# One room for the value products, halves added on load, inverse sums by VectorE: a change to a one-layer hybrid encoder step on Trainium2

## The chip, the cores and the metric

The kernel runs on one core of a Trainium2 chip. A core has TensorE (PE, with its weight loads shown apart as PEld), VectorE (DVE), ScalarE (ACT), GpSimd (POOL) and SyncE (SP, which here only issues transfers), an on-chip memory of 128 partitions (SBUF), the matmul accumulators (PSUM, eight banks), and 16 DMA engines to and from DRAM. The metric is the time of one execution in microseconds (us) on the device; lower is better. Time before: 1430.43 us, median of three runs (1429.32 to 1431.48).

## The reference

One inference step of one layer, for a prompt of 1024 rows and a sample of 64 rows, width 1024, all in fp32:

```
xn = rms_norm(x, g_pre);  z = xn @ w_in          # xa, ga, q, k, v, gb, fl, ma, mb
ya = rg_lru(causal_conv(xa)) * silu(ga)                        # branch A
logf = log_sigmoid(fl + b_f);  cum = cumsum(logf)
s  = q @ k.T * HEAD_DIM**-0.5 + cum[q] - cum[k], masked        # branch B, 16 heads of 64
yb = (softmax(s) @ v) * silu(gb)
u  = [ya, yb] @ w_branch;  mix = sum(sigmoid([ma, mb]) * u) @ w_o
h  = x + rms_norm(mix, g_post)
y  = h + rms_norm(sigmoid(h @ w_ple_gate) * (pe @ w_ple_proj), g_ple)
```

The sample attends to 128 cached rows and itself. Besides y, the step returns k, v, logf and the end states of branch A.

## The kernel before

**Precision.** A matmul operand is split into a high part, rounded to the fast matmul format, and a low part, the remainder. A product takes three passes (high x high, high x low, low x high; lines 179 to 181). ScalarE makes the high part (`copy_act`, line 90), VectorE the low part (`sub`, line 93), so nearly every operand passes both engines, in that order. In the value products of attention, a weight tile holds a value block's high columns (64) beside its low columns (64), so that one pass of 128 output partitions gives "high values" in the lower 64 and "low values" in the upper 64; the two halves have to be added afterwards.

**Stages.** (1) norm, value columns, (2) keys, queries and some other panels by a seven-product scheme (`quad`), (3) attention, mixed with panel products as filler, (4) branch A (convolution, gates, scan), (5) output product of branch A, while branch B's rows come back from DRAM, (6) output product of branch B, (7) w_o, again by seven products, and the last norm and gate.

**Attention.** There are 64 units, each a head and 256 queries (two blocks of 128, called `par` 0 and 1). For a unit:
- `scores` (two matmuls per piece) and `lowest`: VectorE adds the mask and takes the negated maximum,
- `softmax`: ScalarE's exponential with its row sums `sm` (line 1191), GpSimd's power -1 of the sums (line 1193), GpSimd's scaling of the row (line 1194),
- `turn`: four transposes on PE, then ScalarE's high part `th` and VectorE's low part `tl`,
- `values`: matmuls into one half `pv` of a PSUM bank. `pv_half` hands out the two halves of that one bank in turn. After a unit's last value product ScalarE copies the upper 64 partitions to `lo`, VectorE adds the lower 64 from PSUM to it (`y`, line 1293), and GpSimd's queue stores y to DRAM `d_y` (line 1297).

For each of 8 head pairs the sample goes the same way (`sample_scores`, `sample_turn`, `sample_values`): two small copies and two adds out of `pv`, store by SP.

**The order** in attention is worked out while the program is built. PE's instructions are issued in program order, and within attention so are those of ScalarE, VectorE and GpSimd. A planner keeps a clock `now` for PE and, per engine, a list of booked work with estimated costs (the constants `D_MAX`, `A_LO`, `D_Y`, `G_INV`, ...). Of the next score, transpose and value step it takes the first whose due time plus a margin has come (`ready`, `MARGIN`); if there is none it issues one step of a filler panel. The due time of a unit's first value product is also that of a free half: `v_free`, with two entries, one per half. In all other stages PE keeps program order and the other engines' order is worked out by a scheduler when the program is built.

**Branch B's rows.** After attention, `branch_in` (line 1818) loads for each of 8 row blocks k the 128 x 1088 rows `t` of d_y and the rows `z` of d_gb, by SP. `branch_b` gates them: ScalarE's sigmoid of z, VectorE's t * z and t * sigmoid, ScalarE's high part `ybh`, VectorE's low part `ybl`. Rows 0 and 1 are loaded early, before branch A's last scan; rows 2 to 7 share two buffers, so row k + 2 is loaded when row k's low part is done. In the same stage `evac_a` multiplies branch A's products by a gate and stores them to `d_mix` on GpSimd's queue (line 1865, four buffers), and weight panels are loaded by SP and split. Branch B's first panel needs all eight rows within its first 24 matmuls.

Of the kernel before, what the change touches and what calls it, by code (L numbers as in the profile page):

```python
# [8 lines left out]
F32 = mybir.dt.float32  # L9
# [29 lines left out]
GC = 364  # L39

HOP_PE, HOP = 250.0, 90.0
D_MAX, D_LO, D_Y, D_YS = (240.0, 1.035), (130.0, 1.1), 420.0, 230.0
A_EXP, A_HI, A_LO, A_ST, A_W = (450.0, 0.85), (150.0, 0.88), 380.0, 470.0, 1060.0
G_NORM, G_INV = (260.0, 0.84), 220.0
G_DMA = 860.0
D_W = 1240.0

# [26 lines left out]
def hybrid_step(tc, a, o):  # L74
# [958 lines left out]
    def spent(ns):  # L1033
        now[0] += ns
# [21 lines left out]
    def per(cost, n):  # L1056
        return cost[0] + cost[1] * n
# [120 lines left out]
    def tiny2(name):  # L1178
        return p2.tile([P, 1], F32, name=name, tag=name, bufs=12 if name == "nm" else 8)[:, :]

    def lowest(s, w, out, m, least=-NEG):

# [1 line left out]
        return nm, book("D", now[0] + HOP_PE, per(D_MAX, w), lambda: dve.tensor_tensor_reduce(  # L1184
            out=out, in0=s[:, :w], in1=m, scale=-1.0, scalar=least, op0=ALU.add, op1=ALU.min, accum_out=nm))

    def softmax(at, nm, n, pr):


        sm = tiny2("sm")  # L1190
        at = book("A", at, per(A_EXP, n), lambda: act.activation(  # L1191
            out=pr[:, :n], in_=pr[:, :n], func=AF.Exp, scale=-1.0, bias=nm, accum_out=sm))
        at = book("G", at, G_INV, lambda: pool.tensor_tensor(out=sm, in0=sm, in1=warm[:, :], op=ALU.pow))  # L1193
        return book("G", at, per(G_NORM, n), lambda: pool.tensor_scalar(  # L1194
            out=pr[:, :n], in0=pr[:, :n], scalar1=sm, scalar2=1.0, op0=ALU.mult, op1=ALU.mult))

    def width(q2, par):
        n = 256 * q2 + (par + 1) * P
# [4 lines left out]
    def scores(x, i, pr):  # L1203

        h, q2 = units[x]
        t = heads[h]
        half, par = divmod(i, 2)
        n, w = width(q2, par)
        q0 = (2 * q2 + par) * P
        c = slice(half * w, (half + 1) * w)  # L1210
        s = p2s.tile([P, 512], F32, name="s", tag="s")
        pe.matmul(s[:, :w], t["q1"][:, q0:q0 + P], t["k1"][:, c], start=True, stop=False)  # L1212
        pe.matmul(s[:, :w], t["q2"][:HD + 4, q0:q0 + P], t["k2"][:HD + 4, c], start=False, stop=True)  # L1213
        spent(logits_ns(w))
# [39 lines left out]
    lo_free = [0.0]  # L1254
    def values(u, g, h, q2):
        vv = heads_v[h]
        if g == 0:
            pvs[u] = pv_half()
        pv = pvs[u]
        th, tl = turned.pop((u, g))  # L1260
        high = turned_by.pop((u, g))
        def part(j, x, **kw):
            v = vv[:, 2 * g + j, :, :].rearrange("p s d -> p (s d)")
            if g < q2:
                return pe.matmul(pv[:, :256], v, x[:, j * 256:(j + 1) * 256], **kw)  # L1265
            c0 = P if j else 0
            return pe.matmul(pv[:, c0:256], v, x[:, :P] if j else x[:, P:3 * P], **kw)  # L1267

        def high_part(j, stop=False):
            tc.declare_no_dep(part(j, th, start=False, stop=stop).ins, high.ins, reason="ordered through the low part")  # L1270

        if g < q2:
            for j in range(2):
                part(j, tl, start=(g == 0 and j == 0), stop=False)
                high_part(j)
            spent(480.0)
            return
        if q2 == 0:
            part(0, tl, start=True, stop=False)
# [12 lines left out]
        at = book("A", max(now[0] + HOP_PE, lo_free[0]), A_LO, lambda: copy_act(lo[:, :], pv[HD:, :256]))  # L1292
        at = book("D", at, D_Y, lambda: dve.tensor_tensor(out=y[:, :], in0=pv[:HD, :256], in1=lo[:, :], op=ALU.add))
        v_free.popleft()
        v_free.append(at)
        lo_free[0] = at
        book("G", at, G_DMA, lambda: pool.dma_start(dst, y[:, :]))


# [10 lines left out]
    def sample_scores(p):  # L1310
        t = smp[p]
        s = p2s.tile([P, 512], F32, name="s", tag="s")
        three(s[:, :LS], *(x[:, :] for x in qs + t["ks"]), True, False)
        pe.matmul(s[:, :LS], cs_q[:, :], cs_k[:, :], start=False, stop=True)
        spent(440.0)
        nm, at = lowest(s, LS, prs_s[:, :LS], mask_s[:, :])
        return at, softmax(at, nm, LS, prs_s)

    def sample_turn(p):
        t = smp[p]  # L1320
# [9 lines left out]
    def sample_values(p):  # L1330
        t = smp.pop(p)
        pv = pv_half()
        for i in range(2):
            pe.matmul(pv[:, :], t["vs"][:, i, 0, :], t["pt"][:, i, :, :].rearrange("p s n -> p (s n)"),
                      start=(i == 0), stop=False)
            pe.matmul(pv[:, :P], t["vs"][:, i, 1, :], t["pt"][:, i, 0, :], start=False, stop=(i == 1))
        spent(458.0)
        ys = p2.tile([P, DEC], F32, name="ys", tag="ys", bufs=1)
        ats = []
        for j in range(2):  # L1340
            js, ks = slice(j * HD, (j + 1) * HD), slice(P + j * HD, P + (j + 1) * HD)
            ats.append(book("A", now[0] + HOP_PE, per(A_HI, HD), lambda js=js, ks=ks: copy_act(ys[js, :], pv[js, ks])))
        for j, at in enumerate(ats):
            js = slice(j * HD, (j + 1) * HD)
            at = book("D", at, D_YS, lambda js=js: dve.tensor_tensor(out=ys[js, :], in0=pv[js, js], in1=ys[js, :],
                                                                     op=ALU.add))
# [25 lines left out]
    due = {}  # L1372
    s_free = deque([0.0, 0.0, 0.0])
    t_free = deque([0.0, 0.0])
    v_free = deque([0.0, 0.0])
    prs = {}
    seen = {"t": 0, "v": 0}
    last_t = {u: ("t", u, q2) for u, (h, q2) in enumerate(units)}
# [62 lines left out]
            t_free.append(due[step])  # L1441
        done.add(step)

    pool.memset(warm[:, :], -1.0)
    booking = tc.manual_schedule(engines={act.engine, dve.engine, pool.engine})
    booking.__enter__()
    load_head(0)
# [369 lines left out]
        return ybpool.tile([P, T], dt, name=name, tag=f"yb{i}{k}")  # L1817

    def branch_in(k, t, z):
        sp.dma_start(t[:, :], d_y[k])  # L1820
        sp.dma_start(z[:, :], d_gb[k])
        return t, z

# [574 lines left out]
```

## Time and profile before

| | us |
|---|---|
| median of three runs | 1430.43 (1429.32 to 1431.48) |
| the profiled execution | 1429.49 |
| its span, first to last instruction | 1427.5 |
| PE busy | 1410.8 |
| PEld busy | 1358.0 |
| VectorE busy | 899.4 |
| ScalarE busy | 720.5 |
| GpSimd busy | 436.5 |
| granted TensorE clock | 0.998 |

Attention runs from about 453 to 849 us of the span, branch A until about 1046, the output product of branch A with the loading of branch B's rows until about 1111. Busy times of one engine are unions, so a busy PE is one with work in its pipeline. In a row of waits, the instruction named first waited, and the one behind the arrow ended the wait. In a row of time order, the bracket tells how long the engine had been idle before it and what ended that.

### The profile page before, as it was taken

To read this page: it belongs to the slowest core of one execution; us is meant where nothing else is said; L and a number is where in the kernel's file an instruction comes from. 1 tells how busy PE (TensorE), PEld (TensorE's weight loads), DVE (VectorE), ACT (ScalarE), POOL (GpSimd) and SP (SyncE) were. 2 spreads that over 40 slices of the span, in tenths; PEclk is the share of its full clock that TensorE was granted. 3 is DMA by queue.
4 is the path that set the end of the run, shared out by engine and by line. 5 is a ranking of instruction groups with operands and counts; after the bars stand their busy time and mean duration, and the time that the engine had idled before them with its cause. 6 is when DMAs were issued, how large, how long until landed. Compare 5 with 4: busy or idle time off the path is not lost.

```text
span 1427.5 us, 25022 instructions
## 1 busy us (share of the span) xinstructions
PE 1410.8 (99%) x9217; PEld 1358.0 (95%) x9217; DVE 899.4 (63%) x1638; ACT 720.5 (50%) x1339; POOL 436.5 (31%) x652
## 2 busy tenths in 40 slices
PE   9999999999999999999999999999999999999997
PEld 8999999999999999999999999999999999888887
DVE  5564766564432666666666656898767474777654
ACT  5423544442222666666666657777544232565443
POOL 0012322233204777768776841221011000000001
PEclk9999999999999999999999999999999999999999
DMA  6667556765247764556566545564467774224211
GB/s 225 214 133 107 150 155 193 162 180 141 85 122 194 182 130 131 137 110 151 123 150 131 84 101 106 83 101 84 165 211 264 252 237 136 113 74 150 78 48 45
DMA packets 138919, 201.20 MB, mean 141 GB/s; under 512 B 24372, under 2 KB 98844, under 8 KB 137772
## 3 DMA queue, kind: packets, MB, share of 16 engines
q1 hardware_dynamic: 119436, 158.96, 44.2%
q0 software_dynamic: 8160, 23.25, 5.9%
q10 hardware_dynamic: 11200, 17.38, 3.4%
q8 instruction: 73, 1.20, 0.3%
q14 instruction: 50, 0.41, 0.1%
HBM read 131.60 MB, written 66.36 MB: 139 GB/s over the span
## 4 chain that ended last, share of the span: by engine, by line
PE 82%; DVE 6%; DMA 5%; ACT 3%; issue 3%; POOL 1%; SPq 0%; DVEq 0%; ACTq 0%; POOLq 0%
PE quad L844 17%; PE acc L179 11%; PE acc L181 11%; PE acc L180 11%; PE q L2042 5%; PE tp L1244 4%; PE pv L1265 3%; PE s L1213 2%; PE s L1212 2%; PE pv L1267 2%; PE vacc L179 1%; PE vacc L180 1%; PE vacc L181 1%; DMA w_raw<-in_w_in 1%; PE vacc L500 1%
## 5 line engine op out<-in xcount | busy, mean ns | idle before, releaser
L179 PE MATMUL acc<-xh,wh 128*128 128x364 f32 x720 | 237.6, 330 | 0.2 <-ACT st L90 0.2
L181 PE MATMUL acc<-xh,wl 128*128 128x364 f32 x720 | 235.8, 328 | 0.0
L180 PE MATMUL acc<-xl,wh 128*128 128x364 f32 x720 | 235.8, 327 | 0.0
L179 PEld LDWEIGHTS acc<-xh,wh 128*128 128x128 f32 x720 | 135.4, 188 | 1.2 <-ACT st L90 0.5
L180 PEld LDWEIGHTS acc<-xl,wh 128*128 128x128 f32 x720 | 135.3, 188 | 0.8
L181 PEld LDWEIGHTS acc<-xh,wl 128*128 128x128 f32 x720 | 135.1, 188 | 0.0
L90 ACT ACTIVATE wh<-w_raw 128x1024 fp32r<-128x1024 f32 (+1 forms) x66 | 63.4, 962 | 86.4 <-PE quad L844 34.4
L93 DVE TENSOR_TENSOR wl<-w_raw,wh 128x1024 fp32r<-128x1024 f32 (+1 forms) x55 | 62.5, 1138 | 67.6 <-ACT wh L90 47.0
L1193 POOL TENSOR_TENSOR sm<-sm,warm 128x1 f32<-128x1 f32 x136 | 79.2, 582 | 57.0 <-ACT pb L1191 21.8
L93 DVE TENSOR_TENSOR tl<-tp,th 128x512 fp32r<-128x512 f32 x96 | 65.6, 687 | 38.7 <-ACT th L90 37.9
L844 PE MATMUL quad<-xh,wh 128*128 128x272 f32 x416 | 87.4, 291 | 1.8 <-ACT p__3330 L90 1.8
L844 PE MATMUL quad<-xl,wh 128*128 128x272 f32 x416 | 86.1, 288 | 0.0
L844 PE MATMUL quad<-xh,wl 128*128 128x272 f32 x416 | 86.0, 288 | 0.0
L1191 ACT ACTIVATE pb<-pb,nm 128x896 f32<-128x896 f32 (+1 forms) x64 | 63.3, 989 | 24.0 <-DVE nm L1184 21.3
L90 ACT ACTIVATE th<-tp 128x512 fp32r<-128x512 f32 x96 | 56.4, 592 | 31.0 <-PE tp L1244 30.3
L2338 POOL TENSOR_TENSOR junk<-ple,g_ple 128x256 f32<-128x256 f32 x4 | 3.8, 956 | 213.2 <-DVE ple L2295 213.2
L1212 PE MATMUL s<-k,q 128*128 128x128 f32 (+2 forms) x192 | 67.5, 353 | 0.0
L844 PEld LDWEIGHTS quad<-xh,wh 128*128 128x128 f32 x416 | 65.3, 188 | 2.3 <-ACT p__3330 L90 2.0
L1213 PE MATMUL s<-k,q 68*128 68x128 f32 (+2 forms) x192 | 65.3, 344 | 0.5 <-issue 0.5
L844 PEld LDWEIGHTS quad<-xh,wl 128*128 128x128 f32 x416 | 65.5, 188 | 0.0
L844 PEld LDWEIGHTS quad<-xl,wh 128*128 128x128 f32 x416 | 65.4, 188 | 0.0
L1194 POOL TENSOR_SCALAR pb<-pb,sm 128x896 f32<-128x896 f32 (+1 forms) x64 | 61.5, 962 | 6.2
(744 smaller groups left out, 4230.4 us busy)
## 6 DMA issues: line engine op xcount, KB each, us to landing
w_raw<-in_w_in SPq DMA_DIRECT2D x56, 256.0 KB
q<-d_q SPq DMA_DIRECT2D x48, 256.0 KB
k<-d_k SPq DMA_DIRECT2D x48, 256.0 KB
w_raw<-in_w_in SPq DMA_DIRECT2D x64, 128.0 KB
w_raw<-in_w_branch SPq DMA_DIRECT2D x32, 256.0 KB
wl<-w_raw POOLq DMA_DIRECT2D x11, 512.0 KB, 4.5
wraw<-in_w_in SPq DMA_DIRECT2D x20, 256.0 KB
d_k<-oh ACTq DMA_DIRECT2D x16, 272.0 KB
```

The source lines that it names most:

```text
L90: return act.activation(out=out, in_=in_, func=AF.Copy, scale=scale)
L93: return eng.tensor_tensor(out=out, in0=in0, in1=in1, op=ALU.subtract)
L179: pe.matmul(out, ah, bh, start=start, stop=False)
L180: pe.matmul(out, ah, bl, start=False, stop=False)
L181: pe.matmul(out, al, bh, start=False, stop=stop)
L844: pe.matmul(acc[:, c, :CW], l[:, k, :], r[:, k, c * CW:(c + 1) * CW], start=(first and k == 0 and p == 0), stop=(k == 3 and p == 2), skip_ ...
L1191: at = book("A", at, per(A_EXP, n), lambda: act.activation(out=pr[:, :n], in_=pr[:, :n], func=AF.Exp, scale=-1.0, bias=nm, accum_out=sm))
L1193: at = book("G", at, G_INV, lambda: pool.tensor_tensor(out=sm, in0=sm, in1=warm[:, :], op=ALU.pow))
L1194: return book("G", at, per(G_NORM, n), lambda: pool.tensor_scalar(out=pr[:, :n], in0=pr[:, :n], scalar1=sm, scalar2=1.0, op0=ALU.mult, op1 ...
L1212: pe.matmul(s[:, :w], t["q1"][:, q0:q0 + P], t["k1"][:, c], start=True, stop=False)
L1213: pe.matmul(s[:, :w], t["q2"][:HD + 4, q0:q0 + P], t["k2"][:HD + 4, c], start=False, stop=True)
L2042: pe.matmul(acc, l[:, k, :], r[:, k, :], start=(first and k == 0 and i == 0), stop=(k == 3 and i == 2), skip_group_check=not first)
```

## The change

- The planner has one entry for the values' bank (`v_free` with one element). After a unit's last value product one ScalarE copy of 128 x 256 empties it into `y`, and the add on VectorE is gone. GpSimd's queue stores both halves, 128 x 256, to `d_y`, which now has a plane of 128 x 1024 per head.
- In `branch_in` two loads on SP bring the lower halves of the two heads, one brings the sample's rows from `d_ys`, and then two transfers from GpSimd's queue add the upper halves onto the lower ones in SBUF as they land.
- The sample's values are emptied by the same copy, and its two adds read SBUF.
- The sums of a unit's two rows stand side by side in one tile of two columns. After the second exponential one VectorE reciprocal inverts both, and GpSimd then scales the first row and the second. For the sample it inverts one column.
- The planner's costs follow (`INV` 165, `A_Y` 380; `D_Y`, `A_LO`, `G_INV` go).

```
-    d_y = dram.tile([NP, P, T], F32, name="d_y")
+    d_y = dram.tile([NP, 2, P, SEQ], F32, name="d_y")
+    d_ys = dram.tile([NP, P, DEC], F32, name="d_ys")
...
-    def softmax(at, nm, n, pr):
-        sm = tiny2("sm")
-        at = book("A", at, per(A_EXP, n), lambda: act.activation(
+    def powers(at, nm, n, pr, sm):
+        return book("A", at, per(A_EXP, n), lambda: act.activation(
             out=pr[:, :n], in_=pr[:, :n], func=AF.Exp, scale=-1.0, bias=nm, accum_out=sm))
-        at = book("G", at, G_INV, lambda: pool.tensor_tensor(out=sm, in0=sm, in1=warm[:, :], op=ALU.pow))
+    def inverse(at, sm, k):
+        return book("D", at, INV, lambda: dve.reciprocal(out=sm[:, :k], in_=sm[:, :k]))
+    def normal(at, n, pr, sm):
         return book("G", at, per(G_NORM, n), lambda: pool.tensor_scalar(
             out=pr[:, :n], in0=pr[:, :n], scalar1=sm, scalar2=1.0, op0=ALU.mult, op1=ALU.mult))
...
-        return at, softmax(at, nm, n, pr)
+        if par == 0:
+            sm = tiny2("sm", 2)
+            sums[x] = sm, powers(at, nm, n, pr, sm[:, :1]), pr, n
+            return at, at
+        sm, first, pr0, n0 = sums.pop(x)
+        done_ = inverse(max(first, powers(at, nm, n, pr, sm[:, 1:])), sm, 2)
+        return at, normal(normal(done_, n0, pr0, sm[:, :1]), n, pr, sm[:, 1:])
...
-        lo = p2.tile([HD, 256], F32, name="lo", tag="lo", bufs=1)
-        y = p2.tile([HD, 256], F32, name="y", tag="y", bufs=3)
-        dst = d_y[h // 2][(h % 2) * HD:(h % 2 + 1) * HD, q2 * 256:(q2 + 1) * 256]
-        at = book("A", max(now[0] + HOP_PE, lo_free[0]), A_LO, lambda: copy_act(lo[:, :], pv[HD:, :256]))
-        at = book("D", at, D_Y, lambda: dve.tensor_tensor(out=y[:, :], in0=pv[:HD, :256], in1=lo[:, :], op=ALU.add))
+        y = p2.tile([P, 256], F32, name="y", tag="y", bufs=3)
+        dst = d_y[h // 2, h % 2][:, q2 * 256:(q2 + 1) * 256]
+        at = book("A", now[0] + HOP_PE, A_Y, lambda: copy_act(y[:, :], pv[:, :256]))
         v_free.popleft()
         v_free.append(at)
-        lo_free[0] = at
         book("G", at, G_DMA, lambda: pool.dma_start(dst, y[:, :]))
...
-            ats.append(book("A", now[0] + HOP_PE, per(A_HI, HD), lambda js=js, ks=ks: copy_act(ys[js, :], pv[js, ks])))
-        for j, at in enumerate(ats):
-            js = slice(j * HD, (j + 1) * HD)
-            at = book("D", at, D_YS, lambda js=js: dve.tensor_tensor(out=ys[js, :], in0=pv[js, js], in1=ys[js, :],
-                                                                     op=ALU.add))
-        book("D", at, 0.0, lambda: sp.dma_start(d_y[p][:, SEQ:], ys[:, :]))
+            at = book("D", at, D_YS, lambda js=js, ks=ks: dve.tensor_tensor(
+                out=ys[js, :], in0=yv[js, js], in1=yv[js, ks], op=ALU.add))
+        book("D", at, 0.0, lambda: sp.dma_start(d_ys[p], ys[:, :]))
...
-    v_free = deque([0.0, 0.0])
+    v_free = deque([0.0])
...
     def branch_in(k, t, z):
-        sp.dma_start(t[:, :], d_y[k])
+        for j in range(2):
+            sp.dma_start(t[j * HD:(j + 1) * HD, :SEQ], d_y[k, j][:HD, :])
+        sp.dma_start(t[:, SEQ:], d_ys[k])
+        for j in range(2):
+            pool.dma_start(t[j * HD:(j + 1) * HD, :SEQ], d_y[k, j][HD:, :], accum_op=ALU.add)
         sp.dma_start(z[:, :], d_gb[k])
         return t, z
```

More of the change, by code (lines that the diff above doesn't have):

```diff
@@ L41 @@
 HOP_PE, HOP = 250.0, 90.0
-D_MAX, D_LO, D_Y, D_YS = (240.0, 1.035), (130.0, 1.1), 420.0, 230.0
-A_EXP, A_HI, A_LO, A_ST, A_W = (450.0, 0.85), (150.0, 0.88), 380.0, 470.0, 1060.0
-G_NORM, G_INV = (260.0, 0.84), 220.0
+D_MAX, INV, D_LO, D_YS = (240.0, 1.035), 165.0, (130.0, 1.1), 230.0
+A_EXP, A_HI, A_Y, A_ST, A_W = (450.0, 0.85), (150.0, 0.88), 380.0, 470.0, 1060.0
+G_NORM = (260.0, 0.84)
 G_DMA = 860.0
@@ L1176, in load_sample, with tiny2 @@
         t["vs_at"] = book("G", at, 740.0, lambda: sub(pool, vs[:, :, 1, :], v_smp[:, :, :], f(vs[:, :, 0, :])))
-    def tiny2(name):
-        return p2.tile([P, 1], F32, name=name, tag=name, bufs=12 if name == "nm" else 8)[:, :]
+    def tiny2(name, n=1):
+        return p2.tile([P, n], F32, name=name, tag=name, bufs=12 if name == "nm" else 8)[:, :]
     def lowest(s, w, out, m, least=-NEG):
@@ L1185, in lowest @@
             out=out, in0=s[:, :w], in1=m, scale=-1.0, scalar=least, op0=ALU.add, op1=ALU.min, accum_out=nm))
-    def softmax(at, nm, n, pr):
-        sm = tiny2("sm")
-        at = book("A", at, per(A_EXP, n), lambda: act.activation(
+    def powers(at, nm, n, pr, sm):
+        return book("A", at, per(A_EXP, n), lambda: act.activation(
             out=pr[:, :n], in_=pr[:, :n], func=AF.Exp, scale=-1.0, bias=nm, accum_out=sm))
-        at = book("G", at, G_INV, lambda: pool.tensor_tensor(out=sm, in0=sm, in1=warm[:, :], op=ALU.pow))
+    def inverse(at, sm, k):
+        return book("D", at, INV, lambda: dve.reciprocal(out=sm[:, :k], in_=sm[:, :k]))
+    def normal(at, n, pr, sm):
         return book("G", at, per(G_NORM, n), lambda: pool.tensor_scalar(
             out=pr[:, :n], in0=pr[:, :n], scalar1=sm, scalar2=1.0, op0=ALU.mult, op1=ALU.mult))
+    sums = {}
     def width(q2, par):
@@ L1253, in hybrid_step @@
     pvs = {}
-    lo_free = [0.0]
     def values(u, g, h, q2):
@@ L1316, in sample_scores @@
         nm, at = lowest(s, LS, prs_s[:, :LS], mask_s[:, :])
-        return at, softmax(at, nm, LS, prs_s)
+        sm = tiny2("sm", 2)[:, :1]
+        return at, normal(inverse(powers(at, nm, LS, prs_s, sm), sm, 1), LS, prs_s, sm)
     def sample_turn(p):
@@ L1337, in sample_values @@
         spent(458.0)
+        yv = p2.tile([P, 256], F32, name="y", tag="y", bufs=3)
         ys = p2.tile([P, DEC], F32, name="ys", tag="ys", bufs=1)
-        ats = []
+        at = book("A", now[0] + HOP_PE, A_Y, lambda: copy_act(yv[:, :], pv[:, :256]))
+        v_free.popleft()
+        v_free.append(at)
         for j in range(2):
             js, ks = slice(j * HD, (j + 1) * HD), slice(P + j * HD, P + (j + 1) * HD)
-            ats.append(book("A", now[0] + HOP_PE, per(A_HI, HD), lambda js=js, ks=ks: copy_act(ys[js, :], pv[js, ks])))
-        for j, at in enumerate(ats):
-            js = slice(j * HD, (j + 1) * HD)
-            at = book("D", at, D_YS, lambda js=js: dve.tensor_tensor(out=ys[js, :], in0=pv[js, js], in1=ys[js, :],
-                                                                     op=ALU.add))
-        book("D", at, 0.0, lambda: sp.dma_start(d_y[p][:, SEQ:], ys[:, :]))
-        v_free.popleft()
-        v_free.append(at)
+            at = book("D", at, D_YS, lambda js=js, ks=ks: dve.tensor_tensor(
+                out=ys[js, :], in0=yv[js, js], in1=yv[js, ks], op=ALU.add))
+        book("D", at, 0.0, lambda: sp.dma_start(d_ys[p], ys[:, :]))
     units = [(h, q2) for h in range(NH) for q2 in (0, 3, 1, 2)]
@@ L1442, in go @@
         done.add(step)
-    pool.memset(warm[:, :], -1.0)
     booking = tc.manual_schedule(engines={act.engine, dve.engine, pool.engine})
```

## The prediction

> **What bounds the kernel now.** I read the page first, then the busy times by stage, then who waits for whom inside the two stages that the change touches.
>
> ```profile
> PE 1410.8 (99%) x9217; PEld 1358.0 (95%) x9217; DVE 899.4 (63%) x1638; ACT 720.5 (50%) x1339; POOL 436.5 (31%) x652
> ```
>
> ```profile
> 453.00:849.00 396.00, 394.38 (x2739) 383.66 (x2740) 251.19 (x671) 256.14 (x588) 282.18 (x460) 1.00 0.58 131
> 849.00:1046.00 197.00, 196.83 (x1187) 196.53 (x1186) 162.06 (x164) 136.70 (x190) 35.04 (x75) 1.00 0.50 102
> 1046.00:1118.00 72.00, 71.78 (x432) 71.44 (x431) 42.44 (x53) 25.32 (x25) 13.03 (x24) 1.00 0.78 261
> ```
>
> The columns of the second view are the stretch, its length, then busy time (and instructions) of PE, PEld, DVE, ACT and POOL, the granted clock, the DMA share and GB/s. The first row is attention, where score, transpose and value products run with panel products as filler between them. The third is where the output products of branch A run while branch B's rows come back from DRAM and are gated. PE idles 1.62 us in the first and 0.22 us in the third, at full clock. No matmul is added or removed, so the change can win only what PE waits for, and lose by making PE wait. What DVE, POOL and ACT save is worth nothing by itself: none is over 72% busy in attention, and PE's waits there have these names.
>
> ```profile
> PEld pv L1265 <- DVE y L1293: 2.1, 4, 0.7
> PEld pv L1267 <- DVE y L1293: 1.4, 4, 0.4
> PEld pv L1267 <- ACT lo L90: 0.2, 1, 0.2
> PEld pv L1265 <- DVE ys L1345: 0.2, 1, 0.2
> ```
>
> Weight loads run ahead of matmuls, so the wait shows at PEld more fully than at PE (us in total, times, longest). All ten stand at a value product that waits until the values' bank has been emptied: 3.5 us for y, 3.9 us in all. One of them in order of time:
>
> ```profile
> 504.63 0.38 ACT L90 ACTIVATE lo<-pv 64x256 f32<-64x256 f32 x1
> 505.91 0.28 PE L1265 MATMUL pv<-th,vv 128*128 128x256 f32 x1
> 506.29 0.42 DVE L1293 TENSOR_TENSOR y<-pv,lo 64x256 f32<-64x256 f32 x1 [1.95 <-ACT st L90]
> 506.75 0.19 PEld L1267 LDWEIGHTS pv<-diag0l,vv 128*128 128x128 f32 x1 [0.36 <-DVE y L1293]
> ```
>
> ScalarE has copied one unit's upper half, the next unit's products already run in the other half of the bank, the first unit's add then stands between two groups of them, and the second group waits for it. So the two halves are no two rooms: one access at a time goes through.
>
> **The change part by part.** *Emptying the bank.* Rows of what is removed, and the nearest to what is added:
>
> ```profile
> L1293 DVE TENSOR_TENSOR y<-pv,lo 64x256 f32<-64x256 f32 x64 | 26.4, 412 | 32.9 <-ACT lo L90 11.9 <-PE pv L1265 7.8 <-ACT st L90 3.9
> L90 ACT ACTIVATE lo<-pv 64x256 f32<-64x256 f32 x64 | 24.4, 382 | 20.4 <-PE pv L1265 9.4 <-PE pv L1267 7.9 <-PE pv L1336 1.2
> L90 ACT ACTIVATE pts<-tps 128x256 fp32r<-128x256 f32 x8 | 3.0, 379 | 0.1
> L1193 POOL TENSOR_TENSOR sm<-sm,warm 128x1 f32<-128x1 f32 x136 | 79.2, 582 | 57.0 <-ACT pb L1191 21.8 <-DVE diag2l L93 8.1 <-DVE diag0l L93 7.6
> L1297 POOL DMA_DIRECT2D d_y<-y x64 | 37.7, 589 | 28.5 <-DVE y L1293 25.1 <-DVE nm L1184 3.1 <-issue 0.2
> L1194 POOL TENSOR_SCALAR pb<-pb,sm 128x1024 f32<-128x1024 f32 x16 | 18.0, 1122 | 1.5
> L155 DVE RECIPROCAL r_y<-r_y x18: 154/164/165, 5.9 to 1421.8; 128x1 f32<-128x1 f32 x16, 64x1 f32<-64x1 f32 x2
> ```
>
> A copy of 128x256 out of that memory takes 379 ns, one of 64x256 382: the whole copy costs ScalarE what the half does. The 64 adds leave VectorE (26.4 us). For the 8 sample pairs one copy replaces two small ones, and the adds read from SBUF afterwards, off the bank. The bank is now free where lo ends (505.01 in the rows above) and no second reader comes between, so the wait of 0.36 us falls away; the planner, which now knows one room, also puts the next unit's first value product no earlier than 250 + 380 + 90 ns after the last one, less its margin. Its gap is covered by filler, which still runs when attention ends. I take off the 3.5 us of y. Bounds: 3.9 us when the small waits go as well; 0 when ScalarE, whose queue is in order and which waits for maxima before its exponentials, is late with the copy as often as VectorE was with the add.
>
> *Inverse sums.* 136 powers (79.2 us of POOL) go, 72 reciprocals come; the row of 128x1 has 164 ns, so 72 x 0.164 = 11.8 us of VectorE, less than half of what the adds free. A pair of rows is normalised later: after the second exponential stood a power and one scaling (0.58 + 1.12 us at full width), and now 0.16 + 2 x 1.12. That is 0.7 us more, hidden by filler as long as it lasts; PE waits for POOL nowhere in the list above, where POOL was 71% busy, and it will be less. If the cover were gone it would cost up to 64 x 0.7 = 45 us, once per unit; a gain is excluded, as no wait of PE ends on POOL. I take 0.
>
> *Stores.* Each of the 64 stores is of 128 rows instead of 64, which adds 4 MB over 396 us at a DMA share of 0.58; they are read back only after attention has ended. Cost 0, and no gain, since PE waits for no store.
>
> *The load.* A row of branch B was one load of 544 KB. Now it is two loads of 256 KB and one of 32 KB on SP's queue, and behind them two accumulating loads of 256 KB from POOL's queue that wait for the first to land. That is 8 x 0.5 MB more to move, six of the eight rows in the third stage, where the DMA share is already 0.78.
>
> ```profile
> wl<-w_raw POOLq DMA_DIRECT2D x11, 512.0 KB, 4.5
> DMA to landing us min/median/max: 2.1/5.3/7.6
> DMA to landing us min/median/max: 1.9/2.3/11.7
> ```
>
> The first is the only accumulating transfer in the trace, median us from issue to landing; the second and third are the stores of d_mix (182 KB, POOL's queue, in the third stage) and of d_y (64 KB). I take 4.5 + 0.5 (the second issue) = 5.0 us for the pair, because the bytes are the same as in that row. Bounds: 2.8 us if the two halves run side by side at the d_y median; 10.5 us if the crowd adds what it adds to d_mix (7.6 - 2.1 = 5.5). POOL, queued behind the wait, has d_mix's stores (24 in the stage, 4 buffers), for which the sums of branch A wait; with eight banks these have room for the few us in question. Two more issues on SP add 0.8 us. Now the row's own chain. Two buffers: row 5 waits for row 3, row 7 for row 5.
>
> ```profile
> 1059.89 0.44 SPq L1820 DMA_DIRECT2D yb_in<-d_y  x1
> 1060.42 0.37 SPq L1821 DMA_DIRECT2D gb_in<-d_gb  x1
> 1075.11 0.34 SPq L1820 DMA_DIRECT2D yb_in<-d_y  x1
> 1086.65 4.44 SPq L1820 DMA_DIRECT2D yb_in<-d_y  x2
> ```
>
> ```profile
> 1068.18 1.12 ACT L1835 ACTIVATE gb_s<-gb_in 128x1088 f32<-128x1088 f32 x1 [0.19 <-DMA gb_in<-d_gb]
> 1069.42 1.28 DVE L1837 TENSOR_TENSOR yb_in<-yb_in,gb_in 128x1088 f32<-128x1088 f32 x1
> 1073.79 1.29 DVE L93 TENSOR_TENSOR ybl<-yb_in,ybh 128x1088 fp32r<-128x1088 f32 x1 [1.43 <-ACT ybh L90]
> 1083.01 1.22 DVE L93 TENSOR_TENSOR wl<-w_raw,wh 128x1024 fp32r<-128x1024 f32 x1
> 1084.14 1.28 DVE L1837 TENSOR_TENSOR yb_in<-yb_in,gb_in 128x1088 f32<-128x1088 f32 x1
> 1089.46 1.29 DVE L93 TENSOR_TENSOR ybl<-yb_in,ybh 128x1088 fp32r<-128x1088 f32 x1 [0.73 <-ACT ybh L90]
> 1092.31 1.29 DVE L1837 TENSOR_TENSOR yb_in<-yb_in,gb_in 128x1088 f32<-128x1088 f32 x1
> 1101.46 1.28 DVE L1837 TENSOR_TENSOR yb_in<-yb_in,gb_in 128x1088 f32<-128x1088 f32 x1
> 1105.32 1.29 DVE L93 TENSOR_TENSOR ybl<-yb_in,ybh 128x1088 fp32r<-128x1088 f32 x1 [0.73 <-ACT ybh L90]
> ```
>
> ```profile
> 1086.77 0.33 PE L179 MATMUL acc<-yah,wh 128*128 128x364 f32 x1
> 1114.42 0.33 PE L180 MATMUL acc<-ybl,wh 128*128 128x364 f32 x1
> ```
>
> Row 3: its gate, issued at 1060.42, had landed at 1068.18, so loads take 7.8 us here and y landed near 1067.7. With 0.8 + 5.0 it is complete at 1073.5, and the product of 1069.42 moves by 4.1. Row 5 is issued at 1075.11 + 4.1 = 1079.2, lands 7.8 later, is complete at 1092.8: 8.7 later than 1084.14. Row 7 is issued near 1090.8 + 8.7 = 1099.5; row 6's product came 5.7 us after its issue (1086.65 to 1092.31), so it lands by 1105.2 and is complete at 1111.0, 9.5 later than 1101.46. Its low part ends at 1106.61 + 9.5 = 1116.1, and PE takes it at 1114.42: a wait of 1.7 us. At the lower bound of 2.8 the three rows lose 6.6 us less and PE waits for nothing. The other place is the split of weights at 1083.01, needed at 1086.77, 2.5 us to spare, behind row 4's product on VectorE; a shift like row 3's 4.1 costs 1.6 there, and what PE loses there it does not lose again at row 7. I take 1.6 for both.
>
> Sum: 1429.49 (profiled execution, span 1427.5) - 3.5 + 1.6 = 1427.6. The median of the runs is 0.94 above that execution, so 1428.5 as a median.
>
> [...]
>
> **The rivals.**
> - *The loads stay hidden:* accumulates near 2.8 us, by the spare 5 us above. For it: the stage before, with a DMA share of 0.50, takes the two early rows' loads, and only six stand in the crowd. Against it: 4.5 us is measured. 1430.43 - 3.5 = 1426.9.
> - *The rows come late and PE stands before row 7:* one mechanism at one place, the first panel of branch B. Each us that an accumulate takes beyond 5.0 counts three times, for rows 3, 5 and 7. At 8 us, the middle between 5 and 10.5: 1.7 + 9 = 10.7, so 1430.43 - 3.5 + 10.7 = 1437.6. The loss exceeds the gain from 5.6 us on, and is over 0.2% from 6.6. For it: in the same stage d_mix's transfers of a third of the size take 5.3 in the median, and the second product (the sigmoid and split on ScalarE) is in order too. Against it: all the extra bytes of the stage are 6 x 0.52 = 3.1 MB, 12 us at its 261 GB/s, and a chain that slows also thins the crowd.
> - *The bank's waits do not go:* PE waits for ScalarE's copy where it waited for VectorE's add. For it: the lo rows show ScalarE 20.4 us idle before them, so it comes as soon as it can, yet behind other work. Against it: 0.2 us of waits on lo today, though PE's products stood behind lo as well. 1430.43 + 1.6 = 1432.0.
>
> **How the numbers follow.** A measurement of this kernel tells 0.2% (2.9 us) from no change, so the borders are 1427.6 and 1433.3. Forecast 0.40 (1428.5, own range 1427 to 1431, one part in five of it under the border), hidden loads 0.25, late rows 0.25, waits that stay 0.10. Faster: 0.25 + 0.08 = 0.33. Slower: 0.25 + 0.01 = 0.26. No change: 0.41. The range reaches from 1426.3 (3.9 us gained, nothing lost) to 1437.5 (the accumulate at 8 us); the bound of 10.5 in all three rows is left out.
>
> **What would show it.** Waits of PEld for y at L1293's place gone, and none over 0.3 us in total for the copy: the first term. PE's idle time in attention under 0.5 us. In the third stage, a wait of PE or PEld for ybh, ybl or a panel's split, and the last ybl near 1113 (less the 3.5 us); the accumulates' landing near 4.5 us. The prediction is wrong if PE idles over 1 us in attention, if PE waits for POOL's scaling, or if d_mix's stores, held up behind the accumulates on POOL, make PE wait for banks.

## The result, and the profile after

The changed kernel takes 1445.06 us (median, 1442.97 to 1447.82), the kernel before, beside it on the same chip, 1429.88 us: a ratio of 1.0106 (95% interval 1.0086 to 1.0125). The forecast was 1428.5 us, with a range up to 1437.5. The measured time lies outside, on the slow side. The profiled execution took 1445.35 us, its span 1443.6.

First the busy times by stage of the changed kernel (columns as in the prediction: stretch, length, PE, PEld, DVE, ACT, POOL with instructions, clock, DMA share, GB/s):

```profile
453.00:849.00 396.00, 395.96 (x2762) 388.53 (x2763) 241.48 (x681) 248.31 (x581) 205.47 (x331) 1.00 0.61 144
1046.00:1118.00 72.00, 65.36 (x373) 64.08 (x371) 28.05 (x34) 20.11 (x19) 19.92 (x29) 0.95 0.94 261
1118.00:1134.00 16.00, 10.56 (x42) 10.00 (x43) 12.05 (x14) 5.08 (x6) 1.71 (x3) 0.68 0.41 118
```

Attention has won what was forecast: PE issues 2762 products in 396 us where it issued 2739, which is 23 x 0.143 = 3.3 us, and it idles 0.04 us instead of 1.62. All its waits in this stretch, by PE's weight loads:

```profile
PEld s L1218 <- issue: 0.6, 1, 0.6
```

None stands for the copy or for the bank. The loss is in the third stage. Between 1046 and 1134 us PE idles 6.64 + 5.44 = 12.1 us, and for part of the rest it works at a lowered clock (0.95 and 0.68 over the two stretches). These are its waits between the two times (us in total, times, longest):

```profile
PE acc L182 <- DVE wl L93: 8.1, 3, 5.8
PE acc L180 <- ACT wh L90: 1.9, 1, 1.9
PE acc L180 <- ACT ybh L90: 1.2, 1, 1.2
PE acc L181 <- DVE ybl L93: 0.9, 1, 0.9
```

Ten of the twelve us are waits for the two halves of a *weight panel*, not for a row of branch B. By place, 1.4 us stand behind row 2's product, 2.8 behind row 3's halves and 5.8 behind row 6's product; the last 2.1 are row 7 itself. The timeline around the longest shows why (start, duration, engine and line, and in brackets the idle time before):

```profile
1101.75 1.99 SPq L266 DMA_DIRECT2D w_raw<-in_w_branch  x4
1103.79 0.48 SPq L1825 DMA_DIRECT2D yb_in<-d_y  x1
...
1106.09 0.82 POOL L1828 DMA_DIRECT2D yb_in<-d_y  x1 [4.59 <-DMA yb_in<-d_y]
1107.71 0.61 POOL L1873 DMA_DIRECT2D d_mix<-st_a  x1 [0.80 <-DVE st_a L1872]
...
1111.25 1.06 ACT L90 ACTIVATE wh<-w_raw 128x1024 fp32r<-128x1024 f32 x1 [2.14 <-DMA w_raw<-in_w_branch]
...
1111.94 0.86 POOL L1828 DMA_DIRECT2D yb_in<-d_y  x1 [1.20 <-DMA yb_in<-d_y]
...
1118.86 1.29 DVE L1845 TENSOR_TENSOR yb_in<-yb_in,gb_in 128x1088 f32<-128x1088 f32 x1 [8.53 <-DMA yb_in<-d_y]
1120.06 1.22 DVE L93 TENSOR_TENSOR wl<-w_raw,wh 128x1024 fp32r<-128x1024 f32 x1
...
1121.34 0.67 PE L182 MATMUL acc<-ybh,wl 128*128 128x364 f32 x1 [5.76 <-DVE wl L93]
```

The high half of the panel is ready at 1112.31, so VectorE could have made the low half then. But in VectorE's order the gating product of row 6 stands in front of it, and that waits until 1118.86 for the second accumulating transfer. That one was issued at 1111.94, 5.85 us after the first: two stores of d_mix stood between on POOL, and what ended last was the wait for its plain load (issued at 1103.79, behind four loads of weights). From the first accumulate of this row to its product it is 12.8 us. Over all 16 accumulates:

```profile
DMA to landing us min/median/max: 5.2/6.6/10.0
```

At rows 3, 4 and 5 POOL did not stand for the plain load. Its accumulates were issued right behind a store of d_mix, and that store waited for VectorE:

```profile
1082.40 1.29 DVE L1845 TENSOR_TENSOR yb_in<-yb_in,gb_in 128x1088 f32<-128x1088 f32 x1 [6.97 <-issue]
1085.00 0.53 DVE L1872 TENSOR_TENSOR st_a<-acc,gate 128x360 f32<-128x360 f32 x1
1085.83 0.54 POOL L1873 DMA_DIRECT2D d_mix<-st_a  x1 [9.52 <-DVE st_a L1872]
1086.36 1.74 POOL L1828 DMA_DIRECT2D yb_in<-d_y  x2
1094.74 1.29 DVE L1845 TENSOR_TENSOR yb_in<-yb_in,gb_in 128x1088 f32<-128x1088 f32 x1 [5.61 <-issue]
```

Row 3's product stands on VectorE for its accumulates, the sum `st_a` stands behind it, the store of `st_a` holds POOL for 9.52 us, and only then do row 4's accumulates go out, for which row 4's product stands in turn. So the rows are strung together by the order of the work on two engines, VectorE and POOL. By the view of line 1828, these are VectorE's waits for the accumulates (us, times):

```profile
  DVE yb_in L1845: 32.9, 5
```

The clock is the other part. Slices of 2 us around the same wait (the third number from the end is the granted clock):

```profile
1116.00:1118.00 2.00, 0.00 (x0) 0.00 (x0) 0.00 (x0) 0.00 (x0) 0.90 (x2) 1.00 1.07 209
1118.00:1120.00 2.00, 0.00 (x0) 0.00 (x0) 1.15 (x1) 0.00 (x0) 0.00 (x0) 0.60 1.00 223
1120.00:1122.00 2.00, 0.66 (x2) 0.66 (x3) 2.00 (x3) 0.00 (x0) 0.00 (x0) 0.50 0.10 18
1122.00:1124.00 2.00, 2.00 (x9) 2.00 (x8) 2.00 (x3) 1.48 (x2) 0.60 (x1) 0.50 0.00 0
1124.00:1126.00 2.00, 2.00 (x10) 2.00 (x9) 2.00 (x3) 0.63 (x1) 0.00 (x0) 0.69 0.26 93
```

PE stands, the clock falls to 0.50, and after work resumes at 1121.34 a slice touches 9 products, where one at full clock touches 14 (the last row under the long stall below).

### The profile page after: what moved, and what is told of

Same layout as the page of the kernel before. It is cut to its first block, busy times and chain, and to the rows that moved or that the text cites. A ratio compares the mean times of both kernels' runs of the same rounds, so it can differ in the third digit from the quotient of the medians.

```text
span 1443.6 us, 24955 instructions
## 1 busy us (share of the span) xinstructions
PE 1415.7 (98%) x9217; PEld 1364.4 (95%) x9217; DVE 887.5 (61%) x1646; ACT 711.6 (49%) x1331; POOL 372.8 (26%) x531
## 4 chain that ended last, share of the span: by engine, by line
PE 80%; DVE 6%; DMA 5%; issue 4%; ACT 3%; POOL 1%; SPq 0%; DVEq 0%; ACTq 0%; POOLq 0%
PE quad L845 17%; PE acc L180 10%; PE acc L181 10%; PE acc L182 10%; PE q L2050 5%; PE tp L1255 4%; PE pv L1275 3%; PE s L1218 2%; PE s L1217 2%; PE pv L1277 2%; PE vacc L180 1%; PE vacc L181 1%; PE vacc L182 1%; DMA yb_in<-d_y 1%; PE vacc L501 1%
## 5 line engine op out<-in xcount | busy, mean ns | idle before, releaser
L1190 ACT ACTIVATE pb<-pb,nm 128x896 f32<-128x896 f32 (+1 forms) x64 | 63.3, 988 | 20.6 <-DVE nm L1185 19.9
L182 PE MATMUL acc<-ybh,wl 128*128 128x364 f32 (+1 forms) x192 | 64.2, 335 | 5.8 <-DVE wl L93 5.8
L181 PE MATMUL acc<-ybl,wh 128*128 128x364 f32 (+1 forms) x192 | 64.4, 335 | 0.9 <-DVE ybl L93 0.9
```

Of the source, the lines that this page charges most:

```text
L181: pe.matmul(out, ah, bl, start=False, stop=False)
L182: pe.matmul(out, al, bh, start=False, stop=stop)
L1190: return book("A", at, per(A_EXP, n), lambda: act.activation(out=pr[:, :n], in_=pr[:, :n], func=AF.Exp, scale=-1.0, bias=nm, accum_out=sm))
```

## The experiments

**Is the loss in the accumulates alone?** First the changed kernel without them:

```diff
-        for j in range(2):
-            pool.dma_start(t[j * HD:(j + 1) * HD, :SEQ], d_y[k, j][HD:, :], accum_op=ALU.add)
```

> The changed kernel without its 16 accumulating transfers: the rows of branch B hold the lower halves alone, the upper halves are not added, so the output is not the reference's. All else is the changed kernel. Theory A (the whole loss is in how the accumulates make the rows late): the attention gain stays and the third stage is as before, first product of branch A near 1047.4 and of branch B near 1107.3 us, 1426 to 1428 us. Rival B (part of the loss comes from elsewhere, the doubled stores or another order of the instructions): over 1431 us, with waits of PE left in the third stage.

Measured: 1424.32 us, ratio 0.9962 (0.9947 to 0.9977). Its stages:

```profile
1046.00:1118.00 72.00, 72.00 (x435) 72.00 (x433) 42.16 (x51) 26.20 (x26) 10.78 (x20) 1.00 0.82 273
1118.00:1134.00 16.00, 16.00 (x98) 16.00 (x98) 9.24 (x17) 5.53 (x8) 0.00 (x0) 1.00 0.76 281
```

Theory A holds, with a time 1.7 us under its range: whatever else is in the change costs nothing that shows, and the rest of it is a gain of 5.4 us (3.3 to 7.6), of which 3.3 are attention. The rows also price the loss: here PE issues 531 products in the 88 us (the rows add up to 533, as those that cross 1118 stand in both), in the changed kernel 373 + 42 = 415. 116 x 0.166 = 19.3 us are missing; 12.1 are idle, so about 7 went to the lowered clock. The clock itself says nearly the same: it was 0.50 in three stretches of the 88 us, in which PE worked 5.9 + 3.9 + 3.0 = 12.8 us, and at half speed that loses 6.4.

**Is it the accumulating, or the second transfer behind the first?** The same transfers, overwriting:

```diff
-            pool.dma_start(t[j * HD:(j + 1) * HD, :SEQ], d_y[k, j][HD:, :], accum_op=ALU.add)
+            pool.dma_start(t[j * HD:(j + 1) * HD, :SEQ], d_y[k, j][HD:, :])
```

> The changed kernel with the same 16 transfers from POOL's queue, of the same bytes to the same places, behind the same loads, but overwriting instead of accumulating: the lower halves are lost, so the output is not the reference's. Theory A1 (it is the accumulating itself that takes 5 to 9 us): they land in 2 to 4 us, the rows are in time, 1427 to 1433 us. Rival A2 (it is two transfers one after the other, the second issued by POOL only when the first has landed, in a crowded stage): 1442 to 1448 us like the changed kernel, and the issue-to-landing times stay at 5 to 9 us.

Measured: 1442.36 us, ratio 1.0084 (1.0065 to 1.0103). The transfers' time to landing, and PE's main waits:

```profile
DMA to landing us min/median/max: 4.7/7.0/11.1
```

```profile
PE acc L182 <- DVE wl L93: 9.5, 2, 8.6
PE held L180 <- DVE st_a L1872: 4.2, 1, 4.2
```

A2 holds: the transfers that add nothing took as long (7.0 us in the median against 6.6), so here the adding is not what is dear.

**The chain, or the bytes?** One kernel keeps the chain and takes the bytes away; one was meant to keep the bytes in place and take the chain away:

```diff
 acc_thin
-            pool.dma_start(t[j * HD:(j + 1) * HD, :SEQ], d_y[k, j][HD:, :], accum_op=ALU.add)
+            pool.dma_start(t[j * HD:(j + 1) * HD, :DEC], d_y[k, j][HD:, :DEC], accum_op=ALU.add)
 bytes_only
-            pool.dma_start(t[j * HD:(j + 1) * HD, :SEQ], d_y[k, j][HD:, :], accum_op=ALU.add)
+            sp.dma_start(d_up[k, j], d_y[k, j][HD:, :])
```

> The changed kernel with its 16 accumulating transfers in the same places and with the same waits, but each of 64 columns instead of 1024 (16 KB instead of 256 KB); the upper halves of the other columns are left out. Theory H (the chain: a second transfer that POOL may issue only when the first has landed): the latency of a small transfer is 2 us and more, rows still come 3 to 6 us later, 1432 us and more. Theory B (the bytes: 4 MB more through DMA queues that are nearly full in the third stage): 1424 to 1428 us, as without accumulates.

> The changed kernel without accumulates (the upper halves are not added), but with the same 16 x 256 KB moved from the same place at the same point of SP's queue, as copies into a part of DRAM that nobody reads. Nothing waits for them. Theory B (bytes): 1434 us and more, with the rows or the panels of weights landing late and a DMA share near 1.0. Theory H (chain): 1424 to 1428 us.

Measured: acc_thin 1440.62 us, ratio 1.0067 (1.0053 to 1.0081); bytes_only 1423.96 us, ratio 0.9957 (0.9943 to 0.9971). Accumulates of 16 KB, their time to landing and PE's waits:

```profile
DMA to landing us min/median/max: 2.2/6.3/8.9
```

```profile
PE acc L180 <- ACT wh L90: 4.4, 2, 3.5
PE acc L182 <- DVE wl L93: 3.2, 2, 1.8
PE acc L180 <- ACT ybh L90: 2.7, 1, 2.7
```

And where the idle copies of bytes_only went (durations of the issues in ns, then first and last start):

```profile
L1829 SPq DMA_DIRECT2D d_up<-d_y x16: 474/496/850, 497.7 to 849.8; - x16
```

They were issued between 497.7 and 849.8 us, in attention: nothing ties them to the rows' loads, and the schedule moved them there. In the third stage bytes_only is no_accum again (a DMA share of 0.83 and 271 GB/s, against 0.82 and 273). So 4 MB more in attention cost nothing that shows, and the run says nothing of bytes in the crowded stage.

acc_thin does. With a sixteenth of the bytes the median landing falls only from 6.6 to 6.3 us, and of the 20.6 us between the changed kernel and no_accum (by the ratios) 15.0 stay. Theory H holds for these 15.0; the other 5.6 went with the bytes. The time to landing went with the crowd more than with the bytes: in acc_thin's trace the ten accumulates in flight at a DMA share of 0.9 or more took 5.5 to 8.9 us, the six at 0.67 or less 2.2 to 3.5, all of 16 KB. What the chain is made of stays open: in acc_thin and in pool_plain too a row's second transfers stand on POOL both behind its plain loads and behind d_mix's stores, and no run takes these two apart.

**The two buffers.** Rows 2 to 6 loaded into rooms of rows of branch B that are not yet written:

```diff
+    IN = (6, 5, 3, 4, 5, 6, 7)
+    def load_row(k):
+        if k < KT - 1:
+            tz = (row_room(IN[k], i, F32, f"in_{i}{k}") for i in "hl")
...
     def branch_b(k):
-        t, z = branch_in(k, p4.tile([P, T], F32, name="yb_in"), p4.tile([P, T], F32, name="gb_in"))
+        t, z = rows_in.popleft()
```

> The changed kernel with its accumulates, but the rows 2 to 6 are loaded into rooms of rows of branch B that are not yet written (row 7 into a buffer of its own), so no row waits for the buffer of the row two before. Theory A (rows late through the chain of two buffers 3, 5, 7, as my prediction had it): rows land a panel ahead, VectorE does not stand, 1426.5 to 1429.5 us. Rival A3 (the bytes and the read-modify-write crowd the queues whatever the order, and the weight panels come late too): 1438 us and more.

Measured: 1432.26 us, ratio 1.0018 (1.0006 to 1.0030): by the ratios 12.6 us of the loss are gone, though not all, and neither number was met. Its accumulates take no less (median 7.2 us), they only start earlier; eight of the sixteen still lie in the third stage. That stage, and all waits of PE between 1030 and 1134 us:

```profile
1046.00:1118.00 72.00, 70.37 (x411) 69.71 (x412) 41.04 (x49) 24.69 (x24) 20.09 (x32) 0.98 0.87 260
```

```profile
PE held L180 <- DVE st_a L1885: 3.7, 1, 3.7
PE acc L180 <- DVE st_a L1885: 1.1, 1, 1.1
```

The 3.7 us stand at 1042.8, ahead of the third stage: the two early rows' products stand on VectorE, waiting for their accumulates, in front of the first sums of branch A. My prediction had followed only rows 3, 5 and 7. This kernel moves every byte of the accumulates, half of them in the stage, and PE idles 1.6 us there; that is the best evidence here against the bytes, though not a separate test of them.

**The same bytes, loaded plainly by SP, added on an engine.** With the rows in rooms as above:

```diff
-            pool.dma_start(t[j * HD:(j + 1) * HD, :SEQ], d_y[k, j][HD:, :], accum_op=ALU.add)
+            sp.dma_start(t2[j * HD:(j + 1) * HD, :], d_y[k, j][HD:, :])
...
+        pool.tensor_tensor(out=t[:, :SEQ], in0=t[:, :SEQ], in1=t2[:, :], op=ALU.add)   # rooms_dve: dve
```

> The changed kernel with no accumulates: the upper halves are loaded plainly by SP into a tile of their own and added on POOL, with the rows in rooms as in rooms_acc. The bytes of the row loads are those of the changed kernel, without the second transfer waiting for the first. Theory A4 (what costs is the second transfer behind the first, not the bytes): 1425 to 1428 us. Rival A3 (the bytes crowd the stage; weight panels and rows land late anyway): 1431 us and more, with PE waiting for wh, wl or st_a.

> As rooms_pool, with the sum of the two halves on VectorE (eight operations of 128x1024, about 1.2 us each, six of them in the third stage where VectorE is 39 to 59% busy). Theory A4: within 2 us of rooms_pool, no new waits. If VectorE's place in order is what sets the stage even with plain loads: 2 to 6 us slower than rooms_pool, with PE waiting for wl or st_a.

Measured: 1441.42 us, ratio 1.0073 (1.0060 to 1.0086), and 1440.86 us, ratio 1.0058 (1.0042 to 1.0075). A4 is wrong in its number; adding on VectorE cost what adding on POOL did. PE's main wait and, of SP's queue, the waits at the loads of the upper halves and of the weights (rooms_pool):

```profile
PE acc L180 <- ACT wh L90: 8.6, 2, 5.2
```

```profile
SPq L1829 <- PE held L182: 11.9, 1, 11.9
SPq L1829 <- POOL in_h L1844: 7.9, 1, 7.9
SPq L266 <- DMA in_l<-d_gb: 2.9, 1, 2.9
```

A3 gave the better number and named the wait for wh. Its reason, the crowd, is not excluded for these two kernels (the DMA share of the stage is 0.93 and 0.96); against it stands only that rooms_acc moves the same bytes with little loss. By these rows SP stands at the upper halves until the place of their tile is free (11.9 us) or POOL has added (7.9 us), and the weight panels behind, L266, are loaded late. The line of waiting work has moved from POOL and VectorE to SP. That this alone makes the 11 us lost against before was not tried.

**Adding on the way to DRAM.** Lower halves stored plainly, upper halves accumulated onto them one unit later, rows loaded as before:

```diff
-        book("G", at, G_DMA, lambda: pool.dma_start(dst, y[:, :]))
+        more_y()        # pool.dma_start(dst, y[HD:, :], accum_op=ALU.add) of the unit before
+        book("G", at, G_DMA, lambda: pool.dma_start(dst, y[:HD, :]))
```

> The changed kernel, but the halves are added when they are stored: the lower 64 rows are stored plainly and the upper 64 accumulated by POOL onto the same place in DRAM, one unit later, so that a row of branch B is one load as in the kernel before. Theory A (attention gains 3.4 us, all the loss is in the loads): 1425 to 1427 us, no waits of PE in the third stage. Rival E (64 more accumulating transfers on POOL's queue in attention hold up its scalings, and PE waits for them there, or the row loads wait for the last accumulates): 1429 us and more.

Measured: 1484.51 us, ratio 1.0376 (1.0360 to 1.0392). Rival E holds (1429 us and more). PE's largest wait in the whole kernel, and POOL's in attention:

```profile
PE tp L1254 <- POOL pm L1196: 31.5, 12, 14.2
```

```profile
POOL d_y L1268 <- DMA d_y<-y: 68.8, 23, 6.0
```

POOL stands 23 times for a plain store to land, its scalings stand behind, and the transposes wait for these. PE idles 29 us of the 396 there, and its clock is 0.96.

**The inverse sums alone**, on the kernel before (the functions powers, inverse and normal of the change, nothing else of it):

```diff
-        return at, softmax(at, nm, n, pr)
+        if par == 0:
+            sm = tiny2("sm", 2)
+            sums[x] = sm, powers(at, nm, n, pr, sm[:, :1]), pr, n
+            return at, at
```

> The kernel before with only the inverse sums as reciprocals of two rows on VectorE; bank, stores and loads as before. By my prediction's second step: no difference, 1429 to 1431 us, waits for y as before (3 to 4 us). Rival F (VectorE's 11.8 us of reciprocals stand in front of the adds out of the bank, which then come later): 1 to 4 us slower, more waits for y. Rival G (POOL's powers cost PE something that the waits did not show): 1 to 3 us faster.

Measured: 1430.33 us, ratio 0.9997 (0.9988 to 1.0005): no difference, as the second step had it. Its attention:

```profile
453.00:849.00 396.00, 393.84 (x2733) 382.43 (x2732) 258.35 (x742) 255.08 (x588) 207.36 (x322) 1.00 0.58 132
```

POOL is 207 us busy in attention where it was 282, VectorE 258 where it was 251, and PE issues 2733 products where it issued 2739. In the changed kernel the price of the operation is the one taken from the row of before:

```profile
L1194 DVE RECIPROCAL sm<-sm 128x2 f32<-128x2 f32 (+1 forms) x72 | 11.8, 164 | 23.9 <-ACT pb L1190 16.9 <-ACT pm L1190 6.4
```

**The clock by itself.** In the kernel before, one panel of weights is multiplied by 1.0 in place, seven, ten or sixteen times, so that PE stands once:

```diff
+            if ahead[0][0] == ("a", 6):
+                for _ in range(10):        # short_stall 7, long_stall 16
+                    pool.tensor_scalar(out=raw, in0=raw, scalar1=1.0, scalar2=1.0, op0=ALU.mult, op1=ALU.mult)
             halves_of[:] = [copy_act(wh[:, :, :], raw)]
```

> The kernel before, with ten multiplications by 1.0 in place on POOL (about 1.1 us each) ahead of the splitting of one panel of weights of branch A (the panel of column block 6): PE should stand once, for some 5 to 9 us, near 1087 us, in a stage that has full clock in the kernel before. Theory C (a stall of a few us lowers the granted clock afterwards, and this second cost is part of the loss): granted clock of 0.5 to 0.8 for some 8 us behind the stall, and the kernel loses 3 us more than PE stood. Rival D (the low clock of the changed kernel comes from something else, such as its transfers): clock stays 1.00 and the loss equals the stall.

> As one_stall with seven multiplications instead of ten: a stall of some 3 us. If any stall of a few us lowers the clock: a granted clock under 0.9 in the 8 us behind it and 1 us lost beyond the stall. If there is a length below which nothing happens: clock 1.00, loss equal to the stall.

> As one_stall with sixteen multiplications: a stall of some 13 us. If the lowered clock is a fixed restart of some 8 us: about 2 us lost beyond the stall, as in one_stall (6.7 us stood, 8.4 lost between the first product of branch A and the first of branch B). If it grows with the stall: 4 us and more.

Measured: one_stall 1438.85 us, ratio 1.0057 (1.0040 to 1.0073); short_stall 1437.91 and long_stall 1448.90 us, a single run each. The third stage of one_stall:

```profile
1046.00:1118.00 72.00, 65.27 (x381) 64.16 (x380) 41.74 (x48) 24.81 (x24) 25.10 (x33) 0.95 0.69 236
```

of short_stall:

```profile
1046.00:1118.00 72.00, 69.06 (x396) 68.12 (x395) 42.09 (x48) 25.42 (x24) 22.23 (x30) 0.95 0.69 239
```

and of long_stall, with two stretches behind its stall:

```profile
1046.00:1118.00 72.00, 57.84 (x329) 56.73 (x328) 35.47 (x41) 22.33 (x21) 30.08 (x36) 0.88 0.67 231
1102.00:1108.00 6.00, 4.83 (x15) 4.36 (x16) 5.13 (x5) 3.12 (x4) 0.00 (x0) 0.50 0.26 70
1110.00:1112.00 2.00, 2.00 (x14) 2.00 (x13) 1.54 (x2) 0.00 (x0) 0.59 (x1) 1.00 0.85 284
```

Against the 432 products of before (0.167 us each, 0.22 us idle) the three lose 6.0, 8.5 and 17.2 us, in the order short, one, long, while PE idles 2.7, 6.5 and 13.9 us more: 3.3, 2.0 and 3.2 us beyond the stall. (The spans are 8.3, 9.8 and 19.6 us longer than before's; the 1.3 to 2.4 us more were lost ahead of the stage.) Theory C holds: a stall lowered the clock of the stage to 0.95, 0.95 and 0.88 where it otherwise has 1.00, with none of the change's transfers. In these three traces, one of each kernel, the cost beyond the stall didn't grow with it, and short_stall's two breaks of 2.07 and 0.66 us already pay as much as the long one.

**One accumulate a row.**

```diff
-        for j in range(2):
-            pool.dma_start(t[j * HD:(j + 1) * HD, :SEQ], d_y[k, j][HD:, :], accum_op=ALU.add)
+        pool.dma_start(t[:, :SEQ], d_y[k, :, HD:, :], accum_op=ALU.add)
```

> The changed kernel with one accumulating transfer of 512 KB a row instead of two of 256 KB. If the pair is a large part of the loss (its second half stands behind a store of d_mix on POOL's queue): 1436 to 1441 us. If the chain as such (a second stage of transfers, one panel late) is all: 1443 to 1447 us, as the changed kernel.

Measured: 1555.57 us, ratio 1.0885 (1.0866 to 1.0905). Neither expectation. The accumulates' time to landing, and a stretch in which one of them is nearly all that moves:

```profile
DMA to landing us min/median/max: 23.3/25.7/28.9
```

```profile
1150.00:1165.00 15.00, 6.98 (x42) 6.68 (x41) 0.00 (x0) 0.00 (x0) 0.00 (x0) 0.85 0.13 28
```

A DMA share of 0.13 is, of 16 engines, the time of two. With transfers as slow as these the run says nothing of the pair; how much of the loss the stores of d_mix ahead of the accumulates and between them make stays open.

**A version that keeps the gain.** The bank's one copy and the inverse sums stay, and the halves are added on VectorE from the copy in SBUF, so that stores and loads are those of before; sbuf_inplace writes the sum into the copy itself and has four buffers of it (its lines in attention; sbuf_add writes into a tile of its own).

```diff
-        book("G", at, G_DMA, lambda: pool.dma_start(dst, y[:, :]))
+        at = book("D", at, 420.0, lambda: dve.tensor_tensor(out=y[:HD, :], in0=y[:HD, :], in1=y[HD:, :], op=ALU.add))
+        book("G", at, G_DMA, lambda: pool.dma_start(dst, y[:HD, :]))
```

> A version that keeps the one room, its one copy and the inverse sums, but adds the two halves on VectorE from the copy in SBUF, off the bank (64 rows stored, and one load of 544 KB a row, both as in the kernel before). If the gain is the bank's waits alone (theory A): 1425 to 1427 us, faster than both kernels; no waits of PE for the copy in attention and none in the third stage. Rival I (the add on VectorE, 64 times about 0.35 us, holds up the low parts of the transposed blocks, or the copy waits for one of only two buffers): waits for tl, diag or pv in attention, 1428 us and more.

> As sbuf_add, but the sum is written in place into the lower half of the copy, so that there are four buffers of copies instead of two of copies and two of sums. If the buffers kept sbuf_add from its gain (its add waited 2.9 us for a store, and PE stood 2.7 us in the last 49 us of attention): 1425 to 1427 us. If it is VectorE's load (270 us of 396 busy, against 241): 1428 to 1429 us, as sbuf_add.

Measured: sbuf_add 1428.51 us, ratio 0.9987 (0.9978 to 0.9996); sbuf_inplace 1426.78 us, ratio 0.9979 (0.9969 to 0.9988). sbuf_add met rival I's number; sbuf_inplace met the number for the buffers and beats both kernels: 0.21% under before, by the ratios 1.3% under the changed one. Its attention, and all the waits of PE there:

```profile
453.00:849.00 396.00, 394.67 (x2753) 386.64 (x2754) 271.24 (x746) 248.42 (x581) 210.00 (x331) 1.00 0.58 134
```

```profile
PE pv L1274 <- ACT y L90: 1.3, 1, 1.3
PE s L1217 <- DMA k<-d_k: 0.3, 1, 0.3
```

It wins 14 products (2.0 us) of the 23. In both versions one wait of 1.3 us for the copy is left; why was not tried. PE idles 1.3 us in attention here and 3.5 in sbuf_add, at the same load of VectorE (271 and 270 us), which speaks for the buffers; the intervals of the two times overlap, so that the buffers gave the difference is not shown.

## Why the prediction was wrong

*Emptying the bank: right.* Forecast 3.5 us; the trace gives 3.3, the waits for y are gone, none came for the copy. The rival in which they stay falls.

*Inverse sums: right.* 11.8 us of reciprocals as worked out, and no difference in time.

*Stores: right.* Without the accumulates all the rest of the change is faster, 128-row stores included.

*The load: wrong, and all of the error.* The sum had 1.6 us for it; it cost about 19 in the profiled runs. Three things failed.

First, the waits. The step asked when each *row* is needed and found 1.7 us at row 7 and 1.6 at one panel split. It named the split of 1083.01 as standing behind row 4's product, and then counted it once, with a shift of 4.1. But every split in the stage stands on VectorE behind some row, and ScalarE's half behind ybh in the same way. So the price is not lateness beyond a row's due time, it is lateness beyond the few us that a panel's split has to spare, at each row. PE stood 10.0 us for wl and wh and 2.1 for ybh and ybl. Row 7's own wait of 2.1 is near the 1.7 forecast only by luck: its low part was to end at 1116.1 and ended at 1129.0, with PE itself late by then. What the step left out is the other chain, rows 2, 4 and 6: the two buffers tie them as they tie 3, 5 and 7, and the longest wait, 5.8 us, stands behind row 6. It also took each accumulate to be issued as soon as its plain load had landed, and asked only what stands on POOL *behind* the accumulates; at rows 3, 4 and 5 they stood behind a store of d_mix that waited for VectorE. Taking the buffers' chain away (rooms_acc), which lets the loads start earlier, returned 13 us. The early rows, taken as light because their loads lie in a stage with a DMA share of 0.50, are a second place (3.7 us in rooms_acc).

Second, the size. The pair was taken at 5.0 us from a row with the same bytes. Single accumulates took 5.2 to 10.0, median 6.6, and row 6 12.8 from its first issue to its product. "Because the bytes are the same" was the wrong ground: 16 KB took 6.3. The nearer row was the one of d_mix, 5.3 in the median for another size in the same crowd and on the same queue; it was in the fence and served only for a bound.

Third, the clock: no term at all. 6.4 us by the granted clock, about 7 by the missing products, a third of the loss. The slices behind the breaks show 0.50, and in this trace it came not only behind the gap of 5.76 us but also behind gaps of 1.92 and 0.89 us (last section). The profile of before couldn't show it in this stage, where PE idled 0.22 us and the clock was 1.00.

The rival of late rows was nearest in kind and had the right sign, yet it put all waits before row 7 and by its own sum would have needed accumulates of 10.5 us to give 1445. The rival of hidden loads falls. What I had named as signs were the right ones: waits for ybh, ybl and a panel's split came; the accumulates didn't land near 4.5 us. The bytes of the crowd (12 us, by the late rows' sum) were not the main thing: 15.0 of the 20.6 us stay without them (acc_thin).

## What to carry to other kernels

When a transfer is made to wait for another one, follow the instruction that consumes it on its engine and list everything queued behind it: the price is paid by the work with the least slack in that queue, here weight splits, and not by the row that is late. Price a transfer's latency by the rows of the same queue in the same crowd, not by rows of the same size. List also what stands *ahead* of the second transfer on the queue that issues it. And allow for the clock behind a wait of PE: the three stalls here, of 2.7, 6.5 and 13.9 us, cost 3.3, 2.0 and 3.2 us beyond themselves. When an experiment moves work that nobody waits for, look in its trace where the schedule put it.

## What the hardware showed unexpectedly

- The clock fell for breaks that are no single long stall. In the changed kernel two gaps of 1.92 and 0.89 us within 3.5 us (1085.3 to 1088.7) brought 0.50 for some 7 us, and 1.22 and 0.89 us (1126.5 to 1129.1) brought it for 3.4; in short_stall 2.07 and 0.66 us did. A single gap of 1.41 us (the changed kernel) did not, and neither did 0.92 and 1.82 us close together in acc_thin, so the sum of the gaps does not decide it: 2.11 us brought it, 2.74 did not. The stretches at 0.50 lasted 3.4, 6.8 (the changed kernel), 10.2 (pool_plain) and 17.1 us (long_stall), near one, two, three and five times 3.4. What sets them was not shown.
- An accumulating transfer held POOL longer than a plain one of the same shape while it was issued: 0.89 us against 0.53 in the median (the changed kernel and pool_plain).
- The bytes alone did not set a transfer's time. The 512 KB of one_acc, one transfer a row, landed in 23.3 to 28.9 us, at a DMA share of 0.13, where the pair's 256 KB took 5.2 to 10.0 each (the changed kernel). The two differ in how the transfer is cut; what in it made the difference was not shown.
- VectorE added two halves of one SBUF tile that start on different partitions (0 and 64), 64x256 in 0.42 us in the median (sbuf_add), where the add from the bank took 0.41 in the mean (before).
